# V rows of a spatial gating unit in another order on ACT, DVE and POOL

## The chip, the cores and the metric

The kernel runs on one core of a Trainium2 chip. A core has TensorE (PE, matrix products into PSUM), VectorE (DVE), ScalarE (ACT), GpSimd (POOL) and SyncE (SP, which here issues the DMAs). Each engine takes its instructions strictly in the order of its own queue and waits on semaphores for the others. The metric is the time of one execution in microseconds of device time; the time before is the median of three runs.

## The reference

One layer of a decoder on x of 1024 positions by 1024 channels, float32. The part that matters here is the projection and the second of two token mixers, the chunked spatial gating unit:

```python
h = rmsnorm(x, mix_norm)
q, k, v, su, sv, g_a, g_b = split(h @ w_in)       # su, sv: 512 wide, g_a, g_b: 1024
y_att = sliding_window_attention(q, k, v, ...)
u = gelu(su)
v = rmsnorm(gelu(sv), sgu_norm)                   # per position, over 512 channels
mixed[c, i, g] = sum_j tril(w_s[g])[i, j] * v[c, j, g] + b_s[g, i]   # chunks c of 128 positions
y_sgu = u * mixed
x = x + (sigmoid(g_a) * (y_att @ w_oa) + sigmoid(g_b) * (y_sgu @ w_ob)) @ w_out
x = x + conv_gated_mlp(rmsnorm(x, ffn_norm))
```

## The kernel before, in words

Products of float32 are made of three products of float32r parts: a tile is split into a rounded high part (a copy on ACT, `copy_hi`) and a remainder (a subtraction on DVE or POOL). So each operand of TensorE needs one ACT operation and one DVE or POOL operation first. The two gate projections and later the up and down projections use a Strassen-Winograd scheme with seven block products of eight; its right-hand operands `T1` to `T4` are sums and differences of quarter blocks of x (multiplied by its gain), its left-hand ones are sums of weight blocks (`Left.sum_s1` to `sum_s4`, on POOL).

The order of instructions on every engine is written out by hand (`tc.manual_schedule()`); what stands first in the program stands first in the engine's queue. After the attention comes `v_phase` (L773). It goes over eight rows s of 128 positions. TensorE computes two half rows of sv (`v_half(s, 0)` and `v_half(s, 1)`, 24 products of 128x256 each) into a PSUM tile `pvs`. The first halves of rows 0 to 3 are done before the loop. Rows 0 and 1 use the two 1024 wide PSUM buffers `psA`; rows 2 to 7 use four buffers 512 wide, so row 6 takes the buffer of row 2 and row 7 that of row 3 when ACT has read it for the last time. For a row the other engines do in turn:

- `v_gelu(s)` (L734), ACT: GELU into one of two tiles `vg`, then a square whose accumulator is the row's statistic `vss`; the square writes back into `pvs`
- `v_rsqrt(s)` (L740): DVE scales the statistic (L117), POOL raises it to the power -1/2 (L118)
- `v_norm(s)` (L743), DVE: `vg` times statistic times gain
- `v_split(s)` (L746): ACT copies the high part `vsh`, DVE subtracts the remainder `vsl`

The spatial gate has four tiles t of channels in each half of the positions. `sgu_seed(t, half)` (L818) fills a PSUM tile `pm` with the bias on ACT, `sgu_mm` (L824) adds 12 products on TensorE, `sgu_mul` (L832) multiplies u with it on DVE in two operations. `pm` lives in the two `psA` buffers, so seed t+2 waits for the multiplications of t. A tile of the first half needs the remainders of rows 0 to 3.

Between these operations `X_WORK` (L763) places other work by row: the first left-hand weight blocks (`g_left[0]`, its split and sums on POOL), the gain on the second half of x (`x_gain`, ACT), the differences for `T2`, `T3` and `T4` (`x_sums`, DVE) and the split of `T2` (`x_split`). In each row `v_norm` of the row before comes first, then `v_gelu`, then the row's `X_WORK`, then `v_rsqrt`, then `v_split` of the row before.

`first_gate_pair` (L1006) follows: it splits `T3`, does the last gate of the first half (`sgu_mm(3, 0)`), splits the left-hand sums (`w.split_r`, tiles `gax`), and then goes through the first products (`q.prod`, 12 products of 128x512 each), between which the four gates of the second half lie. After it the gate pairs, the merge, the output projection and the convolutional MLP keep TensorE busy to the end.

Of the kernel before, what the change touches and what calls it, by code (L numbers as in the profile page):

```python
# [41 lines left out]
def body(ctx, tc, nc, a):  # L42
    L, H = slice(0, 512), slice(512, 1024)
# [12 lines left out]
    def Y(s, dt=R, shape=None):  # L56
        return big.tile(shape or [128, 4, 1024], dt, tag="Y", name=nm(s), bufs=7)
# [18 lines left out]
    def copy_hi(dst, src, scale=1.0):  # L76
        return nc.scalar.activation(dst, src, AF.Copy, scale=scale)  # L77
# [133 lines left out]
    for k in range(8):  # L211
        x1 = xr[k]
# [156 lines left out]
    def v_split():  # L369

        for g in range(2):
            vg_ = vt[:, :, 64 * g:64 * g + 64]
            vh_, vl_ = vhl[:, :, g, 64 * g:64 * g + 64], vhl[:, :, g, 64 - 64 * g:128 - 64 * g]
            copy_hi(vh_, vg_)
            nc.vector.tensor_tensor(vl_, vg_, vh_.bitcast(F), op=ALU.subtract)
# [162 lines left out]
    def v_half(s, h):  # L538
        if h == 0:
            pvs[s] = PS("pvs")[:, 0:512] if s < 2 else PH("pvs")  # L540
        c = slice(s * 128, (s + 1) * 128)
        for k in range(8):
            mm3(pvs[s][:, 256 * h:256 * h + 256], hx(0, k, c), hx(1, k, c), wv[h][:, 0, k, :],
                wv[h][:, 1, k, :], h == 0 and k == 0, k == 7, skip_group_check=True)
# [57 lines left out]
    xr_raw = []  # L602
# [8 lines left out]
    def sub(eng, out, x, y, op=ALU.subtract):  # L611
        eng.tensor_tensor(out, x, y, op=op)  # L612
        return out

    def x_gain(r, ks):
        for k in ks:
            x = xr_raw[r][:, k, :]
            nc.scalar.activation(x, x, AF.Copy, scale=cp[:, 186 + 4 * r + k:187 + 4 * r + k])

    def x_sums(ks, first):  # L620
        for k in ks:
            x0 = xr_raw[0][:, k, :]
            if first:
                sub(nc.vector, x0[:, L], x0[:, H], x0[:, L])
            else:
                x1 = xr_raw[1][:, k, :]
                sub(nc.vector, x0[:, H], x1[:, H], x0[:, H])
                sub(nc.vector, x1[:, H], x1[:, H], x0[:, L])
                sub(nc.vector, x1[:, L], x1[:, L], x1[:, H])

    assert "".join(FILL).count("u") == 16 and "".join(FILL).count("q") == 12
    man = tc.manual_schedule()
# [107 lines left out]
    def v_rsqrt(s):  # L740
        rsqrt_cols(vss8[:, s:s + 1], vss8[:, s:s + 1], 1, 512)

    def v_norm(s):  # L743
        nc.vector.scalar_tensor_tensor(vg_[s], vg_[s], vss8[:, s:s + 1], sg_b, op0=ALU.mult, op1=ALU.mult)
# [6 lines left out]
    def x_split(n, ks=range(2), eng=None):  # L751
        r, c = {"T1": (0, L), "T3": (0, H), "T2": (1, H), "T4": (1, L)}[n]
        if n not in xb:
            xb[n] = zr[0].tile([128, 2, 4, 512], R, tag="Z", name="T3") if n == "T3" else \
                Y(n, R, [128, 2, 4, 512])
        for k in ks:
            kk = slice(2 * k, 2 * k + 2)
            src = xr_raw[r][:, kk, c]
            copy_hi(xb[n][:, 0, kk, :], src)
            (eng or nc.vector).tensor_tensor(xb[n][:, 1, kk, :], src, xb[n][:, 0, kk, :].bitcast(F),  # L760
                                             op=ALU.subtract)

    X_WORK = {  # L763
        0: lambda: g_left[0].split_p(),
        1: lambda: (x_gain(1, (0, 1)), g_left[0].sum_s3()),
        2: lambda: (x_gain(1, (2, 3)), x_sums((0, 1), False), g_left[0].sum_s1()),
        3: lambda: (x_sums((2, 3), False), g_left[0].sum_s2()),
        4: lambda: g_left[0].sum_s4(),
        5: lambda: x_split("T2", (0,)),
        6: lambda: x_split("T2", (1,)),  # L770
    }

    def v_phase():  # L773
        nc.gpsimd.affine_select(out=wr, in_=wr, pattern=[[0, 8], [1, 128]], compare_op=ALU.is_ge,
                                fill=0.0, base=0, channel_multiplier=-1)
        copy_hi(wgh, wr)
        nc.gpsimd.tensor_tensor(wgl, wr, wgh.bitcast(F), op=ALU.subtract)
        g_left[0].load_p()
        g_left[0].load_q()
        for s in range(n_v[0], 4):  # L780
            v_half(s, 0)
        for s in range(8):
            v_half(s, 1)
            if 4 <= s + 3 < 8:
                v_half(s + 3, 0)
            if s < 4:
                nc.scalar.activation(uT[:, s, :], uT[:, s, :], AF.Gelu_apprx_tanh)
            if s > 0:
                v_norm(s - 1)
            if s > 5:  # L790
                sgu_mm(s - 6, 0)
            v_gelu(s)
            if s in X_WORK and s < 5:
                X_WORK[s]()
            v_rsqrt(s)
            if s == 7:
                sgu_seed(2, 0)
            if s > 0:
                v_split(s - 1)
            if s in X_WORK and s > 4:  # L800
                X_WORK[s]()
            if s == 6:
                sgu_mul(0, 0)
            if s in (4, 5):
                sgu_seed(s - 4, 0)
        sgu_mul(1, 0)
        v_norm(7)
        sgu_seed(3, 0)
        v_split(7)
        sgu_mm(2, 0)  # L810
        sgu_mul(2, 0)


# [4 lines left out]
    def sgu_seed(t, half):  # L818

        pm = pms[t, half] = PS("pm")  # L820
        nc.scalar.activation(pm.rearrange("p (n i) -> p n i", i=128),
                             bs_b[:, t:t + 1, :].to_broadcast([128, 8, 128]), AF.Copy)

    def sgu_mm(t, half):  # L824
        pm = pms[t, half]
        for ci in range(4):
            c = slice(t * 128, (t + 1) * 128)
            g = slice(2 * t, 2 * t + 2)
            mm3(pm[:, ci * 256:(ci + 1) * 256], vs[half][0][:, ci, c], vs[half][1][:, ci, c],
                wgh[:, g, :], wgl[:, g, :], False, True, skip_group_check=True)  # L830

    def sgu_mul(t, half):  # L832
        p4 = pms.pop((t, half)).rearrange("p (c g i) -> p c g i", g=2, i=128)
        for g in range(2):
            r = slice(64 * g, 64 * g + 64)
            u = uT[r, t, 512 * half:512 * half + 512].rearrange("p (c i) -> p c i", i=128)
            nc.vector.tensor_tensor(u, p4[r, :, g, :], u, op=ALU.mult)
# [143 lines left out]
    g_left = [Left(a["wgb"][c], a["wga"][c]) for c in range(8)]  # L981
# [24 lines left out]
    def first_gate_pair():  # L1006

        w, nx = g_left[0], g_left[1]
        psB.__exit__(None, None, None)
        psum["C"] = tc.tile_pool(name="psC", bufs=2, space=bass.MemoryType.PSUM, reuse_waits="tile")  # L1010
        psC = psum["C"].__enter__()
        psum["H"] = None
        psum["P"] = [psC]
        q = Blocks(w.w, xb)
        psum["P"] = [psA]
        x_split("T3", eng=nc.gpsimd)
        sgu_mm(3, 0)
        sgu_seed(0, 1)
        sa_cm.__exit__(None, None, None)
        gates_open()  # L1020
        x1, x7, q.u2 = q.temps()
        w.split_r()
        q.prod(q.v1, "A11", "B11")
        nc.scalar.copy(x1, q.v1)
        sgu_mul(3, 0)
        w.split_s3()
        q.prod(q.g0, "A12", "B21")
        sgu_seed(1, 1)
        sgu_mm(0, 1)
        nc.vector.tensor_tensor(q.g0, x1, q.g0, op=ALU.add)  # L1030
        x_split("T1")
        sgu_mul(0, 1)
        q.prod(q.v1, "S2", "T2", more=True)
        nc.scalar.copy(q.u2, q.v1)
        sgu_seed(2, 1)
        sgu_mm(1, 1)
        sgu_mul(1, 1)
        q.prod(q.v0, "S3", "T3")
        nc.scalar.copy(x7, q.v0)
        sgu_seed(3, 1)  # L1040
        g_left[1].load_p()
        sgu_mm(2, 1)
        sgu_mul(2, 1)
        x_split("T4", eng=nc.gpsimd)
        sgu_mm(3, 1)
        w.split_q(halves=True)
        sgu_mul(3, 1)
        sg_cm.__exit__(None, None, None)
        sums_open()
        e = PS("pe")  # L1050
        psum["P"] = [psA, psA, psC, psC]
        nx.load_q()
        q.prod(q.g1, "S4", "B22")
        nx.split_p()
        q.prod(e[:, L], "S1", "T1")
        nx.sums_q()
        nx.split_s3()
        nc.vector.tensor_tensor(x7, x7, e[:, L], op=ALU.add)
        nc.vector.tensor_tensor(x1, q.u2, e[:, L], op=ALU.add)
        nx.sums_r()  # L1060
        q.prod(q.v0, "A22", "T4", more=True)
        nx.split_q()
        g_left[2].load_p()
        nc.vector.tensor_tensor(q.v1, x7, q.v1, op=ALU.add)
        nc.vector.tensor_tensor(q.v0, q.u2, q.v0, op=ALU.add)
        q.scale(q.zv)
        q.u2 = x1
        return q
# [747 lines left out]
```

## Time and profile before

| | |
|---|---|
| median of 3 runs | 1209.34 us (1208.82 to 1213.22) |
| the profiled execution's own time | 1207.24 us |
| its span, first to last instruction | 1205.5 us |
| PE busy | 1185.8 us (98%) |
| DVE / ACT / POOL busy | 890.2 (74%) / 542.4 (45%) / 573.0 us (48%) |
| mean granted clock of TensorE | 0.998 |
| the rows loop and the gates behind it | about 185 to 258 us |

The span is what lies between the first and the last recorded instruction; the execution's own time is 1.74 us longer. Busy shares are means over the whole span. Times in the rows below count from the start of the span.

### The profile page before, as it was taken

Reading aid. Unit: us, or ns where it says so; the run is one execution under the profiler, and the core shown is the slowest. Engines: PE = TensorE matmul, PEld = TensorE weight load, DVE = VectorE, ACT = ScalarE, POOL = GpSimd, SP = SyncE. Lnnn points to the kernel's source line nnn. Section 1 sums busy time; section 2 is a strip of 40 time slices with the busy share of each in tenths; the row PEclk is TensorE's granted clock in tenths of the full one; section 3 lists DMA queues with packets and bytes.
Section 4 is the critical chain, followed back from the end, with each engine's and each line's share of the span. In section 5 each row is a group of like instructions: output and inputs, shape, how many; then the busy total and the mean of one; then the engine's idle time right before and its main releaser. Section 6 shows DMA issues by size and latency. Waiting matters only on the chain.

```text
span 1205.5 us, 15823 instructions
## 1 busy us (share of the span) xinstructions
PE 1185.8 (98%) x5866; PEld 1002.3 (83%) x5866; DVE 890.2 (74%) x1030; ACT 542.4 (45%) x831; POOL 573.0 (48%) x363
## 2 busy tenths in 40 slices
PE   9999999899999999999999999999999999999998
PEld 8889989888887888888788888888888888888886
DVE  7688966756547666568787888778887788866674
ACT  8455575743335212233545444444444445424331
POOL 2466683478857422243865666657566551000000
PEclk9999999999999999999999999999999999999999
DMA  7010143036787896443132433334242358975471
GB/s 281 23 53 19 54 140 123 18 115 212 252 280 245 326 342 251 160 151 127 47 128 88 143 105 131 110 101 148 97 140 97 114 187 284 386 234 192 145 237 63
DMA packets 78990, 191.27 MB, mean 159 GB/s; under 512 B 8897, under 2 KB 9153, under 8 KB 78913
## 3 DMA queue, kind: packets, MB, share of 16 engines
q1 hardware_dynamic: 78912, 190.26, 45.4%
q8 instruction: 46, 0.75, 0.2%
q14 instruction: 32, 0.25, 0.1%
HBM read 139.63 MB, written 50.59 MB: 158 GB/s over the span
## 4 chain that ended last, share of the span: by engine, by line
PE 84%; DVE 6%; ACT 2%; DMA 2%; issue 1%; POOL 0%; SPq 0%; ACTq 0%; DVEq 0%
PE pz L931 43%; PE pd L1643 10%; PE pdy L1643 7%; PE px L82 2%; PE px L81 2%; PE po L82 2%; PE po L81 2%; PE po L83 2%; PE px L83 2%; DMA ls<-wup 1%; DVE xa L612 1%; PE pv L505 1%; PE pq L81 1%; PE pq L83 1%; PE pq L82 1%
## 5 line engine op out<-in xcount | busy, mean ns | idle before, releaser
L931 PE MATMUL pz<-T,qh 128*128 128x512 f32 x472 | 145.3, 389 | 0.0
L890 POOL TENSOR_TENSOR pl<-lp,ph 128x1024 fp32r<-128x1024 f32 x30 | 73.1, 2437 | 82.9 <-ACT ph L77 82.7
L931 PE MATMUL pz<-B,ph 128*128 128x512 f32 x352 | 109.5, 392 | 0.0
L931 PEld LDWEIGHTS pz<-T,qh 128*128 128x128 f32 x472 | 88.6, 188 | 18.5
L931 PE MATMUL pz<-T,ql 128*128 128x512 f32 x236 | 91.8, 389 | 0.0
L98 POOL TENSOR_TENSOR wjl<-wj,wjh 128x512 fp32r<-128x512 f32 (+1 forms) x24 | 40.8, 1699 | 95.5 <-ACT wjh L77 95.5
L890 POOL TENSOR_TENSOR ql<-lq,qh 128x1024 fp32r<-128x1024 f32 x29 | 75.0, 2587 | 9.1 <-ACT qh L77 9.1
L931 PEld LDWEIGHTS pz<-B,ph 128*128 128x128 f32 x352 | 65.3, 188 | 15.5 <-ACT x L1491 1.8
L946 DVE TENSOR_TENSOR pz<-pz,rstd_b 128x1024 f32<-128x1024 f32 x60 | 73.9, 1232 | 4.6 <-ACT rstd_b L132 2.5
L890 POOL TENSOR_TENSOR s3l<-s,s3h 128x512 fp32r<-128x512 f32 x30 | 41.2, 1372 | 72.7 <-ACT s3h L77 60.4
L931 PE MATMUL pz<-T,s3h 128*128 128x512 f32 x240 | 73.9, 389 | 0.0
L931 PE MATMUL pz<-B,pl 128*128 128x512 f32 x176 | 68.6, 390 | 0.0
L1643 PE MATMUL pd<-bh,ah 128*128 128x512 f32 x176 | 68.5, 389 | 0.0
L1643 PE MATMUL pd<-bl,ah 128*128 128x512 f32 x176 | 68.5, 389 | 0.0
L1643 PE MATMUL pd<-bh,al 128*128 128x512 f32 x176 | 68.5, 389 | 0.0
L931 PE MATMUL pz<-T,AX 128*128 128x512 f32 x264 | 65.1, 397 | 0.0
L931 PE MATMUL pz<-B,AX 128*128 128x512 f32 x264 | 63.4, 389 | 0.0
L931 PEld LDWEIGHTS pz<-T,AX 128*128 128x128 f32 x264 | 50.6, 192 | 10.7
L931 PEld LDWEIGHTS pz<-B,AX 128*128 128x128 f32 x264 | 49.6, 188 | 10.3
L612 DVE TENSOR_TENSOR ls<-ls 128x512 f32<-128x512 f32 x44 | 48.7, 1107 | 12.0 <-DMA ls<-wup 11.2
L1349 DVE SCALAR_TENSOR_TENSOR tv<-pz,cp,tv 128x1023 f32<-128x1023 f32 (+1 forms) x44 | 56.2, 1278 | 0.8
L1349 DVE SCALAR_TENSOR_TENSOR tg<-pz,cp,tg 128x1023 f32<-128x1023 f32 (+1 forms) x44 | 56.2, 1277 | 0.8
(335 smaller groups left out, 3534.4 us busy)
## 6 DMA issues: line engine op xcount, KB each, us to landing
ls<-wup SPq DMA_DIRECT2D x22, 512.0 KB, 5.5
sum<-ls SPq DMA_DIRECT2D x22, 512.0 KB, 4.5
lp<-wup SPq DMA_DIRECT2D x22, 512.0 KB, 3.5
ra<-wdown SPq DMA_DIRECT2D x44, 256.0 KB, 4.4
b<-T SPq DMA_DIRECT2D x44, 256.0 KB, 3.7
B<-tv SPq DMA_DIRECT2D x33, 256.0 KB, 2.0
T<-tt SPq DMA_DIRECT2D x33, 256.0 KB, 2.0
b<-B SPq DMA_DIRECT2D x33, 256.0 KB, 3.2
```

The source lines that it names most:

```text
L81: nc.tensor.matmul(out, wh, mh, start=first, stop=False, **kw)
L82: nc.tensor.matmul(out, wh, ml, start=False, stop=False, **kw)
L83: nc.tensor.matmul(out, wl, mh, start=False, stop=last, **kw)
L98: nc.gpsimd.tensor_tensor(l[:, :nk, :], r[:, :nk, :], h[:, :nk, :].bitcast(F), op=ALU.subtract)
L505: nc.tensor.matmul(o, vhl[:, kb, g, :], w, start=i == 0, stop=i == len(ops) - 1)
L612: eng.tensor_tensor(out, x, y, op=op)
L890: nc.gpsimd.tensor_tensor(l, r, h.bitcast(F), op=ALU.subtract)
L931: nc.tensor.matmul(o, p[:, k, :], y[:, q, k, :], start=not more and k == 0 and j == 0, stop=k == 3 and j == 2, skip_group_check=True)
L946: nc.vector.tensor_tensor(z, z, rstd_b, op=ALU.mult)
L1349: nc.vector.scalar_tensor_tensor(t[:, j:], p[:, 0:1024 - j], cw[:, ci, 2 - j:3 - j], t[:, j:], op0=ALU.mult, op1=ALU.add)
L1643: nc.tensor.matmul(o[d], p[:, k - k0, m], q[:, k - k0, :], start=new and k == 0 and j == 0, stop=k == HK - 1 and j == 2, skip_group_check= ...
```

## The change

`v_split` of the row before now comes directly behind its `v_norm`, ahead of `v_gelu` of the row. `X_WORK` comes ahead of `v_rsqrt` in all rows. The gain on the second half of x is one block in row 2. The last of the three differences of a block (the one for `T4`) goes from DVE to POOL, in rows 3 and 4, as `x_last`. The gates of the first half move one row forward: the products of tile 0 in row 5, 1 in row 6, 2 in row 7; the seeds of tiles 0 and 1 in row 4, of 2 and 3 in rows 6 and 7; the multiplications of 0 and 1 at the start of rows 6 and 7. In the first gate pair the second half of the split of `T3` goes behind the split of the left-hand sums.

```diff
                 sub(nc.vector, x0[:, H], x1[:, H], x0[:, H])
                 sub(nc.vector, x1[:, H], x1[:, H], x0[:, L])
-                sub(nc.vector, x1[:, L], x1[:, L], x1[:, H])
+
+    def x_last(ks):
+        for k in ks:
+            x1 = xr_raw[1][:, k, :]
+            sub(nc.gpsimd, x1[:, L], x1[:, L], x1[:, H])
...
         0: lambda: g_left[0].split_p(),
-        1: lambda: (x_gain(1, (0, 1)), g_left[0].sum_s3()),
-        2: lambda: (x_gain(1, (2, 3)), x_sums((0, 1), False), g_left[0].sum_s1()),
-        3: lambda: (x_sums((2, 3), False), g_left[0].sum_s2()),
+        1: lambda: g_left[0].sum_s3(),
+        2: lambda: (x_gain(1, range(4)), g_left[0].sum_s1(), x_sums((0, 1), False)),
+        3: lambda: (g_left[0].sum_s2(), x_sums((2, 3), False)),
         4: lambda: g_left[0].sum_s4(),
...
+            if s > 5:
+                sgu_mul(s - 6, 0)
             if s > 0:
                 v_norm(s - 1)
+                v_split(s - 1)
+            if s > 4:
+                sgu_mm(s - 5, 0)
             if s > 5:
-                sgu_mm(s - 6, 0)
+                sgu_seed(s - 4, 0)
             v_gelu(s)
-            if s in X_WORK and s < 5:
+            if s == 4:
+                sgu_seed(0, 0)
+                sgu_seed(1, 0)
+            if s in X_WORK:
                 X_WORK[s]()
             v_rsqrt(s)
-            if s == 7:
-                sgu_seed(2, 0)
-            if s > 0:
-                v_split(s - 1)
-            if s in X_WORK and s > 4:
-                X_WORK[s]()
-            if s == 6:
-                sgu_mul(0, 0)
-            if s in (4, 5):
-                sgu_seed(s - 4, 0)
-        sgu_mul(1, 0)
+            if s in (3, 4):
+                x_last((2 * s - 6, 2 * s - 5))
         v_norm(7)
-        sgu_seed(3, 0)
         v_split(7)
-        sgu_mm(2, 0)
         sgu_mul(2, 0)
...
-        x_split("T3", eng=nc.gpsimd)
+        x_split("T3", (0,), nc.gpsimd)
         sgu_mm(3, 0)
         sgu_seed(0, 1)
...
         w.split_r()
+        x_split("T3", (1,), nc.gpsimd)
```

## Rows read from the trace of the kernel before

**Rows 1.** Waits of TensorE: who waited for whom, us in total, times, longest
```profile
PE pm L81 <- ACT pm L821: 4.2, 3, 2.1
```
**Rows 2.** Busy time by stretch: us, PE, PEld, DVE, ACT, POOL, clock, DMA
```profile
184.94:222.54 37.60, 37.60 (x314) 37.40 (x312) 24.30 (x36) 26.22 (x42) 12.01 (x12) 1.00 0.31 112
222.54:229.78 7.24, 3.23 (x25) 3.03 (x26) 5.39 (x10) 4.25 (x7) 0.57 (x2) 1.00 0.01 2
```
**Rows 3.** Timeline of PE: start us, us, operation, [idle before <- releaser]
```profile
184.94 0.28 PE L81 MATMUL pvs<-wvB,x 128*128 128x256 f32 x1
...
216.62 0.28 PE L81 MATMUL pm<-wgh,vsh 128*128 128x256 f32 x1
...
224.44 0.38 PE L81 MATMUL pm<-wgh,vsh 128*128 128x256 f32 x1 [1.90 <-ACT pm L821]
...
228.24 0.39 PE L81 MATMUL pm<-wgh,vsh 128*128 128x256 f32 x1 [2.10 <-ACT pm L821]
...
229.78 0.40 PE L931 MATMUL pz<-x,ph 128*128 128x512 f32 x1
```
**Rows 4.** Timeline of ACT, rows 0 to 5
```profile
188.16 0.69 ACT L737 ACTIVATE vg<-pvs,rstd 128x512 f32<-128x512 f32 x1 [5.09 <-PE pvs L83]
...
189.51 1.04 ACT L77 ACTIVATE ph<-lp 128x1024 fp32r<-128x1024 f32 x1
190.46 1.04 ACT L787 ACTIVATE uT<-uT 128x1024 f32<-128x1024 f32 x1
191.41 0.66 ACT L737 ACTIVATE vg<-pvs,rstd 128x512 f32<-128x512 f32 x1
...
196.21 0.62 ACT L77 ACTIVATE vsh<-vg 128x512 fp32r<-128x512 f32 x1
...
199.31 2.18 ACT L618 ACTIVATE xa<-xa,cp 128x1024 f32<-128x1024 f32 x2
...
203.39 0.69 ACT L737 ACTIVATE vg<-pvs,rstd 128x512 f32<-128x512 f32 x1 [0.43 <-DVE vsl L749]
...
210.38 0.69 ACT L737 ACTIVATE vg<-pvs,rstd 128x512 f32<-128x512 f32 x1 [4.20 <-DVE vsl L749]
...
213.07 1.01 ACT L821 ACTIVATE pm<-rb 128x1024 f32<-128x1024 f32 x1
```
**Rows 5.** Timeline of DVE, in the rows loop
```profile
193.58 1.77 DVE L744 SCALAR_TENSOR_TENSOR vg<-vg,vss,rb 128x512 f32<-128x512 f32 x1 [3.79 <-POOL vss L118]
...
197.79 0.74 DVE L744 SCALAR_TENSOR_TENSOR vg<-vg,vss,rb 128x512 f32<-128x512 f32 x1
198.45 1.40 DVE L612 TENSOR_TENSOR xa<-xa,xa 128x512 f32<-128x512 f32 x2
...
216.95 1.23 DVE L760 TENSOR_TENSOR T<-xa,T 128x1024 fp32r<-128x1024 f32 x1 [0.26 <-ACT T L77]
...
221.93 1.39 DVE L837 TENSOR_TENSOR uT<-pm,uT 64x512 f32<-64x512 f32 x2
```
**Rows 6.** Timeline of POOL, in the rows loop and behind it
```profile
192.98 0.56 POOL L118 TENSOR_TENSOR vss<-vss,mh 128x1 f32<-128x1 f32 x1
193.49 1.30 POOL L612 TENSOR_TENSOR s<-lp,lq 128x512 f32<-128x512 f32 x1
...
234.47 2.42 POOL L890 TENSOR_TENSOR gax<-lr,gax 128x1024 fp32r<-128x1024 f32 x1
236.85 2.27 POOL L890 TENSOR_TENSOR s3l<-s,s3h 128x512 fp32r<-128x512 f32 x1
```
**Rows 7.** PE after its wait at 578 us and in the first gate pair; clock
```profile
580.08 1.95 PE L1322 MATMUL pz<-ones,sq 128*128 128x2 f32 x16 [1.79 <-DVE sq L1442]
...
581.89 4.35 PE L931 MATMUL pz<-T,AX 128*128 128x512 f32 x11
...
236.68 2.92 PE L931 MATMUL pz<-T,gax 128*128 128x512 f32 x12
...
582.40:585.70 3.30, 3.30 (x10) 2.58 (x9) 2.11 (x4) 0.00 (x0) 3.30 (x3) 0.52 0.00 0
```

## Prediction

> **What bounds the kernel now.** I read the waits of TensorE first, then its busy time by stretch, then the instructions of every engine in the stretch that the change touches. TensorE is the bound: it is busy for 1185.8 of 1205.5 us, so what happens on ACT, DVE and POOL counts only where TensorE waits for it. The largest single group of its waits is for the seeds of the spatial gate, `pm` on ACT: 4.2 us in three waits [rows 1]. They lie behind the rows loop. From 184.94 to 222.54 us TensorE is never idle, and in the next 7.24 us it works 3.23 [rows 2]. The two idle pieces are 1.90 us before `sgu_mm(2,0)` and 2.10 us before `sgu_mm(3,0)`; the first gate product then starts at 229.78 [rows 3]. Each seed waits for the two multiplications of the product two tiles earlier, because `pm` has only two PSUM buffers, and those multiplications stand late in DVE's order. So at most 4.2 us can be won here, and all work behind 229.78 keeps TensorE full: a shift of that start reaches the end unless a later stall swallows it.
>
> For the loss I need TensorE's own pace. Eleven half rows take 216.62 - 184.94 = 31.68 us, 2.88 each [rows 3]. Rows 1 to 4 have two (5.76 us), rows 5 to 7 one.
>
> **Prices.** ACT: GELU, square and its accumulator read of a row 1.35 (188.16 to 189.51), the row's `vsh` copy 0.62 long, a gain 1.09, a seed 1.0 long, a 1024 wide copy 1.04 long; the next ACT instruction starts about 0.1 before the end of the one ahead of it (190.46 behind 189.51) [rows 4]. DVE: a subtraction 0.7, a T2 split 1.2, a pair of gate multiplications 1.4, `v_norm` 0.74, but 1.77 where a POOL sum starts 0.1 us before it; that sum still takes its 1.30 [rows 5, 6]. POOL: the power 0.55, a sum or difference 1.3, a 1024 wide remainder, as half a T split, 2.4 [rows 6].
>
> **The edits, step by step** (all times on the axis of the trace of before).
>
> *`v_split` moves ahead of `v_gelu`.* Before, GELU of row s stood ahead of the copy of row s-1, and ACT took it as soon as TensorE had the row: GELU(1) at 191.41, copy 0 only at 196.21 [rows 4]. After, copy s-1 stands ahead of GELU(s), and it needs `v_norm(s-1)` on DVE, which needs the power on POOL, which needs the square of row s-1. That closes a loop through four engines' queues: 1.35 (GELU to statistic) + 0.15 + 0.55 + 0.74 + 0.6 is at least 3.4 us a row, with 0.3 us of hand-overs 3.7, and everything that stands between in these queues is added. Behind the waiting copy on ACT stand GELU, seeds, gains and T2 copies.
>
> Row 1: the power of row 0 and `v_norm(0)` lie where they lay, DVE 193.58 to 195.35 [rows 5]. Copy 0 at 195.4, GELU(1) at 195.9, not 191.41. The sum s1 on POOL starts with `v_norm(1)`, which ends at 199.9.
> Row 2: copy 1 at 200.0, GELU(2) 200.5, then four gains to 206.1. DVE's four subtractions (203.0 to 205.85) stand ahead of the statistic of row 2, so the power runs at 206.1 and `v_norm(2)` beside the POOL sum from 206.6 to 208.5.
> Row 3: copy 2 at 208.5, GELU(3) 209.05 (before: 203.39 [rows 4]), its square done at 210.4. `pvs(7)` takes the buffer of `pvs(3)` (six tiles, four buffers), and TensorE reaches it at 184.94 + 8 x 2.88 = 208.0: **2.4 us idle**, where there was none.
> Row 4: four subtractions to 212.6, statistic, power, then `v_norm(3)` beside the first of the moved differences on POOL, to 215.3. GELU(4) at 215.85; both seeds stand behind it, the first is done at 218.2. TensorE has finished row 5 at 216.15 and `sgu_mm(0,0)` is now in row 5: **2.1 us idle**. The second pair of moved differences lies beside `v_norm(4)`, to 220.7.
> Row 5: GELU(5) 221.25; T2 copy, T2 split and only then the statistic at 224.8; multiplication 0 on DVE to 226.3, `v_norm(5)` to 227.05.
> Row 6: copy 5, seed 2 done 228.65, where TensorE is through row 7 at 226.9: **1.8 us idle** before `sgu_mm(2,0)`. GELU(6) 228.6, T2 copy 229.9, T2 split to 232.2, multiplication 1 to 233.6, `v_norm(6)` to 234.4.
> Row 7: copy 6, seed 3 done 236.0; `sgu_mm(2,0)` ended at 230.1, so **5.9 us idle** before `sgu_mm(3,0)`. Both waits that the change aims at are still there, the second nearly three times as long: GELU(6) to GELU(7) now takes 7.3 us, TensorE's row there about 4.3.
>
> *First gate pair.* The first product starts at 237.4. GELU(7), statistic, power, `v_norm(7)` and `v_split(7)` end at 240.2, multiplication 2 at 241.6, the seed behind it on ACT at 242.65, then the copy of `gax`, then POOL's 2.42 for its remainder [rows 6], to 246.1; TensorE has done two products (5.5) and one gate (1.44) by 244.3: **1.5 to 1.8 us idle**. Without the second T3 half behind `gax` this would be 2.4 more, so that edit helps. The other T3 half and the S3 remainder, 2.27 beside T1 on DVE [rows 6], cost about **0.5**, a seed late behind T1's split **0.8**.
>
> *`x_last` on POOL.* Four differences leave DVE (4 x 0.7 = 2.8 us) and become 4 x 1.3 = 5.2 us on POOL. T4 is needed only in the first gate pair, so POOL's own time is free; their price is the three DVE operations that wait beside them, counted above. From both sides: nothing if none overlaps, 5.2 if DVE waits out all four. The gains as one block on ACT cost nothing new beyond row 2; the wait for x's second load disappears, but nobody is late by it. No DMA is added or passed by another.
>
> The Trainium skill, page "SBUF — State Buffer", section "Who interferes with whom", says that a DVE operation with two SBUF inputs and a POOL operation that reads SBUF exclude each other, whichever starts first keeping the port throughout. The pairs of 1.77 and 1.30 agree [rows 5, 6]. By that rule the four differences on POOL do not relieve DVE of their time; without the rule the sum would be the +4 of the third case below.
>
> **Sum.** New idle time 2.4 + 2.1 + 1.8 + 5.9 + 1.6 + 0.5 + 0.8 = 15.1; old idle time in its place 4.2. That is +10.9. The same queue rules, applied to the old order, give 5.0 us of waits where the trace has 4.2, so they are about 0.6 too dear here, and I take +10.3. The profiled execution took 1207.24 us (span 1205.5 and 1.74 around it): 1217.5. The median of the runs is 2.1 above that execution, which would give 1219.6; I forecast between, **1218.5**.
>
> The clock is a further cost. After 1.79 us of idling and two of tiny products, TensorE ran at 1.2 instead of 2.4 GHz for some 3.3 us, and twelve products took 4.35 for eleven of them against 2.92 for twelve [rows 7]: about 1.7 us lost. The 4 us of idling in two pieces around 226 left the clock full [rows 2]. The Trainium skill, page "TensorE: Matmul & The Clock Gate", section "Why this matters for your kernels", says that long gaps between bursts bring the half clock back. By that rule the 5.9 us gap costs 1.7 more in the products behind it; no row shows so long a gap. Whether it comes or not, the sum keeps its value, for those products run into the wait for `gax`, which is as long.
>
> **Rivals.**
> *A, the forecast*, 0.70: the loop through four engines sets rows 3 to 7.
> *B, nothing queues*, 0.08: copies and norms come early enough, seeds are ready, the 4.2 us go: 1207.24 + 1.3 (half of the gap to the median) - 4.2 = 1204.5. For it: the seeds and the gates do stand earlier in all orders, and the wait of GELU for the old remainder (4.20 us at 210.38 [rows 4]) is gone. Against it: GELU(6) would have to be through by 222, so each row's loop would have to fit into 4.3 us with the T2 work of 2.2 in it; from 3.7 a row upward that fails. It decides where DVE takes the T2 split after the statistic or ACT takes GELU before the copy; neither order is written so.
> *C, no exclusion between POOL and DVE*, 0.12: the norms take 0.74 throughout, the buffer of `pvs(3)` is free in time and row 5 is not late. Left are 0.7 before `sgu_mm(2,0)`, 5.9 before `sgu_mm(3,0)`, 1.5 at `gax`, 0.3: 8.4 - 4.2 = +4.2, 1212.7. Against it stand the 1.77 rows.
> *D, more than counted*, 0.10: the row buffers bind one row earlier as well (0.3 to 0.7), hand-overs of 0.1 more per step, half clock that is not hidden (1.7): +14, 1222.5.
>
> Something under 0.5% of the time, 6 us, is what a measurement of this kernel cannot tell from no change. A and D lie beyond it except for a small part of A; C and B within it. Chances: faster 0.02, same 0.20, slower 0.78. Range 1212 to 1224: it leaves out B below and a little of D above.
>
> **What would show it.** Right: TensorE idle before the second half of `pvs(7)` at about 208 us on a wait for ACT's square, one long wait of 5 to 6 us before the fourth gate, ACT waiting in each row for DVE's `v_norm` ahead of the `vsh` copy, GELU to GELU 7 us in rows 5 to 7, first gate product at 237 and not 229.8. Wrong: GELU(3) before 206 (then the buffer is free in time), `v_norm` at 0.74 beside POOL's differences, or a first gate product before 232.

## The result and the profile after

The changed kernel takes 1219.12 us in the median of five executions, the kernel before beside it 1210.11. The ratio is 1.0062 (95% interval 1.0041 to 1.0083): slower by some 7.5 us (0.0062 x 1210; interval 5.0 to 10.0). The forecast was 1218.5. (One of the five executions took 1259.43 at a granted clock of 0.891 and is in no comparison; the median of the other four is 1218.09.) The profiled execution took 1219.35 us with a span of 1217.6, that is 12.1 more than the span before.

The first lines of the page show that TensorE's busy time rose too, from 1185.8 to 1190.5 us, with the same 5866 products. So not all of the loss is waiting.

```profile
span 1217.6 us, 15819 instructions
PE 1190.5 (98%) x5866; PEld 1006.4 (83%) x5866; DVE 891.1 (73%) x1026; ACT 541.9 (45%) x831; POOL 578.5 (48%) x367
```

TensorE's waits (who waited for whom, us in total, times, longest) answer to [rows 1]. The seeds now cost 9.5 us instead of 4.2, and a wait for the square of ACT in `pvs` is new. The last row lies at the very start of the kernel: the change doesn't touch it, it is 0.4 us or less in some profiles, where the loop then starts at 184.76 to 185.10, and 1.5 to 1.8 in others, with a start at 185.70 to 186.09. Here it starts everything 1.15 us later (186.09 instead of 184.94).

```profile
PE pm L81 <- ACT pm L822: 9.5, 4, 5.7
PE pvs L81 <- ACT pvs L742: 2.2, 1, 2.2
...
PE pkv L81 <- ACT x L77: 1.7, 1, 1.7
```

The timeline of TensorE (start, us, operation, idle before it and what ended that) answers to [rows 3]. In order: first product of the rows loop; first half row of `pvs(7)`; `sgu_mm(0,0)`, `(2,0)`, `(3,0)`; first gate product; `gax` product; a product with the S3 remainder; third gate of the second half; first product of the next gate pair.

```profile
186.09 0.28 PE L81 MATMUL pvs<-wvB,x 128*128 128x256 f32 x1
...
211.50 0.39 PE L81 MATMUL pvs<-wv,x 128*128 128x256 f32 x1 [2.21 <-ACT pvs L742]
...
218.96 0.39 PE L81 MATMUL pm<-wgh,vsh 128*128 128x256 f32 x1 [1.45 <-ACT pm L822]
...
229.26 0.39 PE L81 MATMUL pm<-wgh,vsh 128*128 128x256 f32 x1 [1.41 <-ACT pm L822]
...
236.68 0.58 PE L81 MATMUL pm<-wgh,vsh 128*128 128x256 f32 x1 [5.73 <-ACT pm L822]
...
239.41 1.05 PE L932 MATMUL pz<-x,ph 128*128 128x512 f32 x2
...
246.80 2.91 PE L932 MATMUL pz<-T,gax 128*128 128x512 f32 x12
...
251.63 0.50 PE L932 MATMUL pz<-T,s3l 128*128 128x512 f32 x1
...
255.15 0.38 PE L81 MATMUL pm<-wgh,vsh 128*128 128x256 f32 x1 [0.95 <-ACT pm L822]
...
266.31 0.62 PE L932 MATMUL pz<-x,ph 128*128 128x512 f32 x2
```

ACT's timeline (to [rows 4]) shows who is late. Each `vsh` copy (L77) waits for DVE's `v_norm`, and each GELU (L741) follows behind it, in the last two rows behind a seed as well: 197.07, 210.03, 229.14, 236.56. From GELU(6) to GELU(7) it takes 7.42 us.

```profile
196.53 0.63 ACT L77 ACTIVATE vsh<-vg 128x512 fp32r<-128x512 f32 x1 [3.88 <-DVE vg L748]
197.07 0.67 ACT L741 ACTIVATE vg<-pvs,rstd 128x512 f32<-128x512 f32 x1
...
209.49 0.63 ACT L77 ACTIVATE vsh<-vg 128x512 fp32r<-128x512 f32 x1 [1.24 <-DVE vg L748]
210.03 0.67 ACT L741 ACTIVATE vg<-pvs,rstd 128x512 f32<-128x512 f32 x1
...
227.66 0.63 ACT L77 ACTIVATE vsh<-vg 128x512 fp32r<-128x512 f32 x1 [3.57 <-DVE vg L748]
228.20 1.01 ACT L822 ACTIVATE pm<-rb 128x1024 f32<-128x1024 f32 x1
229.14 0.67 ACT L741 ACTIVATE vg<-pvs,rstd 128x512 f32<-128x512 f32 x1
...
235.08 0.63 ACT L77 ACTIVATE vsh<-vg 128x512 fp32r<-128x512 f32 x1 [3.56 <-DVE vg L748]
235.61 1.01 ACT L822 ACTIVATE pm<-rb 128x1024 f32<-128x1024 f32 x1
236.56 0.67 ACT L741 ACTIVATE vg<-pvs,rstd 128x512 f32<-128x512 f32 x1
```

On DVE (to [rows 5]) stands one turn of that loop. The T2 split waits for its copy behind GELU(6) on ACT; the statistic, the multiplication and `v_norm(6)` stand behind the split. And `v_norm(3)` beside a moved difference takes 1.77, `v_norm(6)` beside nothing 0.75. The second fence is POOL's timeline (to [rows 6]): the two moved differences of row 3, and the S3 remainder far behind them.

```profile
214.23 1.77 DVE L748 SCALAR_TENSOR_TENSOR vg<-vg,vss,rb 128x512 f32<-128x512 f32 x1 [0.66 <-POOL vss L118]
...
231.55 1.23 DVE L764 TENSOR_TENSOR T<-xa,T 128x1024 fp32r<-128x1024 f32 x1 [2.53 <-ACT T L77]
232.69 0.15 DVE L117 TENSOR_SCALAR vss<-vss 128x1 f32<-128x1 f32 x1
232.87 1.39 DVE L838 TENSOR_TENSOR uT<-pm,uT 64x512 f32<-64x512 f32 x2
234.29 0.75 DVE L748 SCALAR_TENSOR_TENSOR vg<-vg,vss,rb 128x512 f32<-128x512 f32 x1
```

```profile
214.16 2.99 POOL L612 TENSOR_TENSOR xa<-xa 128x512 f32<-128x512 f32 x2
...
249.31 2.27 POOL L891 TENSOR_TENSOR s3l<-s,s3h 128x512 fp32r<-128x512 f32 x1
```

The windows (us, busy PE, PEld, DVE, ACT, POOL, then granted clock, DMA share, GB/s) give the clock: behind the wait for `pvs(7)`, late in and behind the long wait, and behind a wait of 1.79 us far later. At 0.50 TensorE runs at 1.2 GHz instead of 2.4.

```profile
211.50:214.00 2.50, 2.50 (x21) 2.50 (x22) 2.03 (x4) 0.00 (x0) 0.36 (x1) 1.00 0.03 7
...
234.00:236.00 2.00, 0.00 (x0) 0.00 (x0) 1.27 (x3) 0.92 (x2) 0.00 (x0) 0.50 0.00 0
...
236.68:240.70 4.02, 4.02 (x16) 3.79 (x17) 1.33 (x3) 2.35 (x5) 0.55 (x1) 0.53 0.03 6
240.70:246.80 6.10, 6.10 (x34) 5.26 (x33) 3.72 (x6) 4.81 (x7) 4.64 (x2) 1.00 0.00 0
...
592.00:598.60 6.60, 6.60 (x21) 5.54 (x21) 3.82 (x6) 0.00 (x0) 6.60 (x5) 0.50 0.00 0
```

**Where the 12.1 us came from.** I measure a *stretch* in every profile: from the first product of the rows loop to the first product of the next gate pair behind the seven here. Before it takes 70.15 us (184.94 to 255.09, the row below), after 80.22 (186.09 to 266.31): +10.07. The late start adds 1.15. The other 0.9 lies behind the stretch.

```profile
255.09 0.62 PE L931 MATMUL pz<-x,ph 128*128 128x512 f32 x2
```

### The profile page after: what moved, and what is told of

Its sections match the earlier page's. It is cut to its first block, busy times and chain, and to the rows that moved or that the text cites. A ratio compares the mean times of both kernels' runs of the same rounds, so it can differ in the third digit from the quotient of the medians.

```text
span 1217.6 us, 15819 instructions
## 1 busy us (share of the span) xinstructions
PE 1190.5 (98%) x5866; PEld 1006.4 (83%) x5866; DVE 891.1 (73%) x1026; ACT 541.9 (45%) x831; POOL 578.5 (48%) x367
## 4 chain that ended last, share of the span: by engine, by line
PE 80%; DVE 7%; ACT 3%; issue 2%; POOL 2%; DMA 1%; SPq 0%; ACTq 0%; DVEq 0%; POOLq 0%
PE pz L932 42%; PE pd L1645 10%; PE pdy L1645 7%; PE px L83 2%; PE px L81 2%; PE po L81 2%; PE po L83 2%; PE po L82 2%; PE px L82 2%; DMA ls<-wup 1%; PE pq L81 1%; PE pq L83 1%; PE pq L82 1%; DVE ls L612 1%; DVE vg L748 1%
## 5 line engine op out<-in xcount | busy, mean ns | idle before, releaser
L932 PEld LDWEIGHTS pz<-B,AX 128*128 128x128 f32 x264 | 49.6, 188 | 10.3
```

Of the source, the lines that this page charges most:

```text
L932: nc.tensor.matmul(o, p[:, k, :], y[:, q, k, :], start=not more and k == 0 and j == 0, stop=k == 3 and j == 2, skip_group_check=True)
```

## The experiments

The theory: the copy of row s-1 ahead of GELU(s) closes a loop through ACT, DVE and POOL that is slower than TensorE's row, and the seeds behind it come late. The rivals are a cost of the gates' new places, of the differences on POOL, of `X_WORK` ahead of the statistic, or of the half clock. "Stretch" is always against 70.15. Ratios are against the kernel before on the same chip (median 1207.93 us for the first four runs, 1208.55 for the next four, 1209.56 for the last).

**The split back in its old place.**

```diff
                 v_norm(s - 1)
-                v_split(s - 1)
...
             v_rsqrt(s)
+            if s > 0:
+                v_split(s - 1)
```

> The changed kernel with one part undone: v_split of the row before stands behind v_rsqrt again, as it did. Queue theory (the copy of row s-1 ahead of GELU(s) closes a loop through ACT, DVE and POOL that is longer than TensorE's row): TensorE no longer waits for the buffer of pvs(3) near 209 us, the wait before sgu_mm(3,0) falls from 5.7 to about 4.4, one wait of about 1.7 before sgu_mm(0,0) is left, now for v_split(3); sum about 4 us above before, 5.5 to 6 below the changed kernel. Rival 1 (POOL's differences hold up DVE): little changes, 8 to 10 us above before. Rival 2 (the gates came forward before their inputs were there): 8 us or more above before.

Measured: 1211.28 us, ratio 1.0033 (1.0018 to 1.0048) where the changed kernel has 1.0062, stretch 74.37: +4.22. So the split's place carries 5.85 of the 10.07 (some 3.5 us by the runs); the 4.22 left are near what the gates alone cost (below). The wait for `pvs` is gone, as expected. The wait of 1.7 that was expected before `sgu_mm(0,0)` did not come, and the one before `sgu_mm(3,0)` fell to 5.06 only, not to 4.4:

```profile
229.22 0.58 PE L81 MATMUL pm<-wgh,vsh 128*128 128x256 f32 x1 [5.06 <-ACT pm L823]
```

**The split alone, in the kernel before.**

```diff
                 v_norm(s - 1)
+                v_split(s - 1)
...
-            if s > 0:
-                v_split(s - 1)
             if s in X_WORK and s > 4:
```

> The kernel before with one part of the change: v_split directly behind v_norm, ahead of GELU; nothing else. Queue theory: 7 us above before, 2.2 of it at the buffer of pvs(3) near 208 us, and one long wait of 8 to 9 us before sgu_mm(2,0), whose seed stands behind GELU(7). Rival 1: no change, nothing was added on POOL. Rival 2: no change, the gates lie where they lay.

Measured: 1215.42 us, ratio 1.0075 (1.0056 to 1.0095), stretch 79.27: +9.12, 2 more than expected. This one move makes nearly the whole loss, in the runs as in the stretch (0.0075 x 1208 = 9.1). The waits are the two foreseen, the new one for `pvs` and a long one, here before `sgu_mm(2,0)`, 7.63 and not 8 to 9. The middle row is the product behind the 24 that waited for `pvs`:

```profile
210.29 0.39 PE L81 MATMUL pvs<-wv,x 128*128 128x256 f32 x1 [1.99 <-ACT pvs L738]
...
214.76 0.28 PE L81 MATMUL pvs<-wvB,x 128*128 128x256 f32 x1
...
234.06 0.58 PE L81 MATMUL pm<-wgh,vsh 128*128 128x256 f32 x1 [7.63 <-ACT pm L820]
```

**The last difference back on DVE.**

```diff
-            sub(nc.gpsimd, x1[:, L], x1[:, L], x1[:, H])
+            sub(nc.vector, x1[:, L], x1[:, L], x1[:, H])
```

> The changed kernel with the four last differences on DVE again, in the same places of the program. Queue theory: the same time as the changed kernel to within 0.5 us (about 10 above before): v_norm(3) and v_norm(4) take 0.74 or wait less, but DVE has 2.8 us of work more in the same loop; the wait before sgu_mm(0,0) grows from 1.5 to 2.5, that before sgu_mm(2,0) shrinks by as much. Rival 1: 4 us above before, 6 below the changed kernel. Rival 2: no change against the changed kernel.

Measured: 1215.55 us, ratio 1.0070 (1.0049 to 1.0092), stretch 79.55, 0.67 below the changed kernel; by the runs the two can't be told apart. `v_norm(3)` still takes 1.78 there, now beside a POOL sum of weights; `v_norm(4)` takes 0.75. The waits fell by more, to 9.81 (2.20 + 1.90 + 4.77 + 0.94) from 11.75 (2.21 + 1.45 + 1.41 + 5.73 + 0.95). What ate the rest is the clock: behind the wait of 1.90 it fell to half, and the slower products used up the wait before `sgu_mm(2,0)`. The first fence is its timeline, the second its windows.

```profile
219.40 0.39 PE L81 MATMUL pm<-wgh,vsh 128*128 128x256 f32 x1 [1.90 <-ACT pm L822]
```

```profile
220.00:221.00 1.00, 1.00 (x7) 1.00 (x6) 0.48 (x1) 0.78 (x2) 0.00 (x0) 0.50 0.00 0
```

**The statistic ahead of the other work.**

```diff
+            v_rsqrt(s)
             if s in X_WORK:
                 X_WORK[s]()
-            v_rsqrt(s)
```

> The changed kernel with v_rsqrt ahead of X_WORK in every row, so that the statistic and the power no longer stand behind the subtractions and T2's split on DVE. Queue theory: the loop is shorter in rows 2 and 3, the buffer of pvs(3) is free in time and its 2.2 us go; in rows 5 to 7 the T2 copy and the gate's multiplication still stand in it, so the wait before sgu_mm(3,0) stays at 5.7; sum about 7.5 us above before, 2.4 below the changed kernel. Rival 1: no change against the changed kernel. Rival 2: no change against it either.

Measured: 1213.94 us, ratio 1.0062 (1.0040 to 1.0084), stretch 78.81: 1.41 below the changed kernel, 1.0 short of the expected gain. The ratio is that of the changed kernel, so by the runs this gain is not shown; it stands in one profile. The wait for `pvs` is gone as foreseen. But TensorE reached `sgu_mm(0,0)` earlier and waited there for 3.22 us instead of 1.45, and behind that the clock fell to half. Row 7 is no faster: 5.17 us before the last gate.

```profile
217.00 0.38 PE L81 MATMUL pm<-wgh,vsh 128*128 128x256 f32 x1 [3.22 <-ACT pm L822]
...
233.99 0.58 PE L81 MATMUL pm<-wgh,vsh 128*128 128x256 f32 x1 [5.17 <-ACT pm L822]
```

```profile
219.00:221.00 2.00, 2.00 (x12) 2.00 (x11) 1.15 (x2) 1.97 (x5) 2.00 (x2) 0.50 0.83 262
```

**The gates alone, in the kernel before.**

```diff
+            if s > 5:
+                sgu_mul(s - 6, 0)
             if s > 0:
                 v_norm(s - 1)
+            if s > 4:
+                sgu_mm(s - 5, 0)
...
+            if s == 4:
+                sgu_seed(0, 0)
+                sgu_seed(1, 0)
...
-        sgu_seed(3, 0)
         v_split(7)
-        sgu_mm(2, 0)
```

> The kernel before with only the gates of the first half one row forward (products in rows 5 to 7, seeds and multiplications as in the changed kernel); v_split, X_WORK, x_last and T3 as before. Queue theory: it is slower too, by about 3.4 us: the first gate waits some 1.5 for v_split(3), which stands behind the statistic in row 4, the wait before sgu_mm(3,0) is about 3 and the product on gax waits some 3, since T3's two halves stand ahead of it. So the gates' part is a third of the loss, and the order of v_split the larger one. Rival 2 (gates forward are the cause): 8 to 10 us above before. Rival 3 (the gates forward alone are the gain that was meant, and only v_split spoils it): 2 to 4 us below before.

Measured: 1211.62 us, ratio 1.0031 (1.0019 to 1.0044), stretch 73.61: +3.46. The two waits of 1.90 and 2.10 of [rows 3] became one of 4.39, behind which the clock was at half, as it had not been behind the two short ones. Then the products with `gax`, behind both halves of `T3` here, wait 1.44. In sum 1.83 more waiting (4.39 + 1.44 - 4.00) and 1.55 of slow products (2.14 for the gate and 6.41 from there to the next, before 1.54 and 5.46). The sum of 3.4 was expected, its parts were not: no wait at the first gate, where 1.5 was expected, 4.39 for 3, and 1.44 for 3.

```profile
229.40 0.39 PE L81 MATMUL pm<-wgh,vsh 128*128 128x256 f32 x1 [4.39 <-ACT pm L819]
...
241.46 2.57 PE L929 MATMUL pz<-T,gax 128*128 128x512 f32 x10 [1.44 <-POOL gax L888]
```

```profile
230.20:233.70 3.50, 3.50 (x14) 3.06 (x13) 1.90 (x4) 2.08 (x5) 0.55 (x1) 0.52 0.02 5
```

9.12 and 3.46 make more than 10.07. As I read it, both edits delay the same seeds and only the later one counts; no run separates this.

**TensorE kept busy in the long gap**, in the changed kernel, with products that nobody reads.

```diff
         v_split(7)
+        warm_up = PH("warm")
+        for _ in range(46):
+            nc.tensor.matmul(warm_up[:, 0:256], vs[0][0][:, 0, 0:128], wgh[:, 0:2, :], start=True, stop=True)
```

> The changed kernel with 46 products of 128x256 into an unused PSUM tile between sgu_mm(2,0) and sgu_mm(3,0), 5.5 us of TensorE work in the wait of 5.7 us; they compute nothing that is used. The clock stays full. Theory of a hidden clock: TensorE leaves the two products behind the gate some 1.8 us earlier, and waits that long for gax instead; the stretch as a whole keeps its time to within 0.4 us. Rival: 1.8 us faster than the changed kernel, the half clock is paid in full.

Measured: 1216.70 us, ratio 1.0075 (1.0053 to 1.0097), stretch 80.20 against 80.22. The clock stayed at 1.00 behind the gap and the first gate product came 1.19 us earlier in the stretch (52.13 us after its beginning, not 53.32), but then the `gax` products waited 0.69 for ACT's copy of an earlier product, into whose PSUM tile they write, and 0.31 for the remainder of `gax`. So in the changed kernel the half clock costs nothing of its own.

```profile
229.81 5.68 PE L814 MATMUL warm<-wgh,vsh 128*128 128x256 f32 x46
...
244.99 0.73 PE L935 MATMUL pz<-T,gax 128*128 128x512 f32 x2 [0.69 <-ACT x L1029]
...
246.03 2.58 PE L935 MATMUL pz<-T,gax 128*128 128x512 f32 x10 [0.31 <-POOL gax L894]
```

**The same with the split alone.**

```diff
+        warm_up = PH("warm")
+        for _ in range(58):
+            nc.tensor.matmul(warm_up[:, 0:256], vs[0][0][:, 0, 0:128], wgh[:, 0:2, :], start=True, stop=True)
         sgu_mm(2, 0)
```

> The kernel before with v_split ahead of GELU, and 58 products of 128x256 into an unused PSUM tile ahead of sgu_mm(2,0), 7.0 us of TensorE work in its wait of 7.6; they compute nothing that is used. There the products behind the wait do not run into another one, so the half clock is paid: 1.8 us faster than without them, 7.3 us above before in this stretch instead of 9.1. Rival: no change against it, then the excess of 1.8 us over the queue rules has another cause.

Measured: 1215.03 us, ratio 1.0062 (1.0039 to 1.0084), stretch 77.78: 1.49 less than the split alone, where 1.8 was expected. The ratios, 1.0062 and 1.0075, can't show a difference of this size. The clock stayed at 1.00 behind the gap, where in the split alone it was at 0.50 from 231.7 to 238.4. There no wait for `gax` follows, so the half clock is paid. The one behind the wait for `pvs` is not: `sgu_mm(2,0)` starts 49.10 us into the stretch with it and 49.11 without. Without the half clock the split alone costs 7.63, near the 7 expected above.

**Another order.** If the loop is the cause, an order that takes GELU(s) ahead of the copy of row s-1, the statistic right behind the square, each subtraction and T2 half in a gap of its own and the multiplications and seeds early should beat both kernels. The loop over rows is replaced by one written list of single operations; the first gate product also goes ahead of `sgu_mm(3,0)`.

```diff
-        for s in range(8):
-            v_half(s, 1)
...
+        for n in V_ORDER:
+            if not n.startswith("acc"):
+                v_step(n)
...
+        "sq2 vsh1 vsl1 acc2 s1b L117_2 gain2 s2a pl pow2 gelu3 s2b sq3 acc3 L117_3 norm2 vsh2 pow3 "
...
-        x_split("T3", (0,), nc.gpsimd)
+        q.prod(q.v1, "A11", "B11")
+        x_half("T3", 0, "l", nc.gpsimd)
         sgu_mm(3, 0)
```

> A new order from the changed kernel: GELU(s) ahead of the copy of row s-1, statistic and power directly behind the square, v_norm(s) already in row s, subtractions, T2 copies and splits spread singly over rows 2 to 6, multiplication and seed ahead of v_norm in rows 5 to 7, the last differences on POOL, the left-hand splits a little later, and the first gate product of the first pair ahead of sgu_mm(3,0). By queue rules with the durations of the traces TensorE waits only 0.2 to 1 us in this stretch: 4 to 5 us below before, some 14 below the changed kernel. Rival 1 (POOL's differences): 1 to 4 us above before, waits before sgu_mm(0,0) and (2,0). A loss would say that waits on three engines at once have hand-overs that the rules miss.

Measured: 1208.08 us, ratio 0.9996 (0.9981 to 1.0011), stretch 71.50: +1.35, not the gain expected. The waits for seeds fell to 0.70, but TensorE now waited 0.90 for `pvs` and 2.31 before the first gate product, which takes the buffer of row 7's square:

```profile
204.32 0.39 PE L81 MATMUL pvs<-wv,x 128*128 128x256 f32 x1 [0.90 <-ACT pvs L812]
...
228.48 0.73 PE L991 MATMUL pz<-x,ph 128*128 128x512 f32 x2 [2.31 <-ACT pvs L812]
```

**That order again, gains later, row 7's GELU earlier.**

```diff
+        "ugelu0 vh01 vh11 gelu0 vh40 sq0 acc0 vh21 L117_0 gelu1 vh50 pow0 norm0 vh31 s3 sq1 s1 "
+        "acc1 ph seed00 L117_1 gain1 vsh0 pow1 gain2 gain3 ugelu2 s1a pl norm1 s2a vsl0 gelu2 s2b "
+        "sq2 gain0 acc2 vh60 vsh1 s3a s3b s2c L117_2 pow2 vh41 vsl1 gelu3 sq3 s0a s1b norm2 acc3 "
...
+        "T2l1 seed20 mm20 mul10b T3h1 vsh6 gelu7 sq7 vsl6 acc7 L117_7 pow7 T3h0 mul20a seed30 "
+        "norm7 vsh7 mul20b vsl7 "
```

> e7's order with its two misses mended: the gains take the blocks of x in the order 1, 2, 3, 0 and start later, since the last block landed only at 199 us there, and row 7's GELU and square are earlier against TensorE, since the first gate product waits for their PSUM buffers. By queue rules with the durations of the traces TensorE waits only some 0.5 us in this stretch: 4 us below before in the stretch, 3 to 5 in the runs. If hand-overs are worse than the rules, the stretch is 0 to 2 us below before and the runs show no difference. The other theories (POOL's differences cost 5 us, gates a row forward cannot be fed) expect a loss of 1 to 4.

Measured: 1205.77 us, ratio 0.9977 (0.9964 to 0.9990): faster than both kernels, by 2.8 us against the one before. But its stretch is 70.14, no shorter. It still has 1.93 us before the first gate product, with half clock behind it (0.55 from 226.85 to 230), and 0.67 at a later gate.

```profile
226.85 0.98 PE L991 MATMUL pz<-x,ph 128*128 128x512 f32 x2 [1.93 <-ACT pvs L812]
```

In its profile the gain lies behind: a wait of 1.56 us that the kernel before has at 376.72 (for a tile of x at L1082) is not there. That wait need not belong to the order: it is 0.2 to 1.9 us in seven of the other profiles and absent in two. So what the 2.8 us of the runs come from stays open. That the spread order would win inside the stretch has failed as a forecast, twice: without the loop the 10 us are gone, but the 4 us of before are not won.

## Why the prediction was right, point by point

The mechanism held. It is the first rival, A. The signs listed as proof stand in the traces: the wait for `pvs(7)` (before its first half, not its second as the prediction says), one wait of 5 to 6 us before the fourth gate, `vsh` waiting for `v_norm`, a row of 7 us.

**The loop, row by row.** On the axis of before (1.15 less) GELU(1) starts at 195.92 (predicted 195.9), GELU(3) at 208.88 (209.05), GELU(6) at 227.99 (228.6). GELU(6) to GELU(7) is 7.42 (7.3). The queue rules were too dear by 0.6 over six rows, which is what the sum took off. The first gate product starts at 238.26 (237.4), late by the half clock in front of it. The split alone, in the kernel before, shows cause and not only company.

**The five waits of TensorE.** Predicted 2.4, 2.1, 1.8, 5.9 and 0.8 (13.0), measured 2.21, 1.45, 1.41, 5.73 and 0.95 (11.75). Against the old 4.2 that is +7.55.

**The S3 remainder (0.5).** It is in no list of waits, but in the timelines: POOL ends it at 251.58, and the first product with it starts at 251.63, 0.65 behind the start of the two before it. Before the change that is 0.47. The twelve S3 products take 3.06 from start to end of their turn, before 2.75: +0.31.

**The wait for `gax` (1.6).** It does not appear as a wait. In its place stands the half clock: the sixteen products from `sgu_mm(3,0)` on (its twelve and the first four of the gate) took 4.02 us at 0.53. The fourth gate, from its first product to the gate product, takes 2.73 where before it took 1.54 (229.78 - 228.24 [rows 3]): +1.19. The two gate products behind it take 5.96 (239.41 to 245.37), before 5.46: +0.50, in all 1.69. That the clock would fall and that it would hide in the wait for `gax` was in the prediction; the run with TensorE kept busy shows it. The Trainium skill, page "TensorE: Matmul & The Clock Gate", section "Why this matters for your kernels", has long gaps bring the half clock back; the gap of 5.73 agrees.

**The sum.** 7.55 of waits, 1.69 of half clock and 0.31 at S3 make 9.55 of the 10.07. The 0.5 left is what a wait costs besides its idle time. Neighbouring products of 0.28 start 0.12 apart (24 in 2.88); where TensorE has waited, this overlap of 0.16 is lost, and the first product takes 0.39 and the next starts 0.22 behind it, together about 0.25 a wait. There are five waits where there were three (1.90, 2.10 and one of 0.18). The +10.3 was near, partly by errors that cancel: 0.65 too much for the five waits (13.0 - 4.2 - 0.6 = 8.2 against 7.55) and 0.2 for S3, against the 0.5 that it left out; the half clock stands for the wait at `gax`, 1.69 for 1.6, as it had allowed. Two slips in its figures weigh little: 5.0 against 4.2 makes its rules 0.8 too dear, not 0.6, and the 1.3 that it adds for the rivals is more than half of the gap of 2.1. The start and the 0.9 behind the stretch were not in it. By the runs the change costs 5 to 10 us, by the stretch of one profile 10.07, so the runs bear out the size only to some 2.5 us.

**`x_last` on POOL.** The norms of rows 3 and 4 take 1.77 and 1.78 beside the differences, as the forecast had it, so the third rival, C, is out by its premise; the exclusion stands in every run, so its price of +4.2 is untested. What the move itself costs was priced too high, as three slowed DVE operations: with the differences on DVE the stretch is 0.67 shorter, DVE has four more operations of 0.7, and row 7's loop is as long. The Trainium skill, page "SBUF — State Buffer", section "Who interferes with whom", says that such a pair exclude each other; 1.77 beside a difference against 0.75 beside none agrees.

**The gates a row forward.** The prediction priced them only inside the loop. By themselves they cost 3.46, nearly half of it in slow products behind the one long wait into which they join two short ones. This was its gap: it took the two seed waits of before as a loss to be won back, and not also as two waits that left the clock full. That the second `T3` half behind `gax` saves 2.4, as it says, no run tests by itself.

**The rivals B and D.** B (nothing queues) falls with GELU(6) at 227.99, where it needed 222. D (+14) would have needed a half clock that isn't hidden; that is what the split alone shows (1.49), but not the changed kernel.

## What to carry to other kernels

Where engines work in order, write down for each row the loop that the queues close (here ACT copy, GELU, square, DVE statistic, POOL power, DVE norm, ACT copy) with everything that stands between, and compare it with the bound engine's time per row: 7.4 against 4.3 us decided this case, and moving one copy ahead of one GELU closed the loop. Removing an upstream wait (`pvs(7)`, 2.21 us) moves it downstream as long as the loop itself is not shorter (1.77 of it came back at `sgu_mm(0,0)`). And before a clock loss is added to a sum, look at what waits behind it: it cost nothing where TensorE had to wait for an operand anyway, and 1.5 us where it hadn't.

## What the runs showed of the hardware that was not expected

Waits of about 2 us left the clock in two states. In the changed kernel the 2.21 us before `pvs(7)` left it full (the window from 211.50, above). In the run with TensorE kept busy, the same wait behind the same work halved it for 3.2 us, and the slower products used up the 1.45 before `sgu_mm(0,0)`; its window:

```profile
211.40:214.60 3.20, 3.20 (x16) 3.20 (x16) 2.50 (x4) 0.00 (x0) 1.95 (x3) 0.50 0.02 5
```

The split alone and the same with TensorE kept busy make another such pair, again one program up to the added products: behind 1.99 us the 24 products took 4.47 us (210.29 to 214.76, above), behind 1.98 us they took 2.98, at full clock:

```profile
210.00:213.00 3.00, 2.92 (x24) 2.92 (x25) 2.86 (x6) 0.03 (x1) 0.00 (x0) 1.00 0.02 5
```

Likewise 1.90 and 2.10 us one after the other left it full before [rows 2, 3], and one of 1.90 halved it in the run with the differences on DVE.

At the `ones,sq` product both kernels wait 1.79 us; before, the half clock lasts 3.3 us [rows 7], after 6.6 (the window from 592.00, above). Those 3.3 us more at half clock lose 1.65, more than the 0.9 that the changed kernel is longer behind the stretch. So a wait of about 2 us was followed by no slow products at all or by up to 6.6 us of half clock, half of which is lost. In the two pairs the program up to the wait is the same, so the order of the instructions does not decide it alone; what does isn't shown.
